# Gate and up of the second FFN: two pairs of blocks by seven part products in place of eight (Strassen's algorithm)

## The chip, the cores and the metric

The kernel runs on one core of one Trainium2 chip. Its time is the device time of one execution in microseconds; the median of the runs is quoted. Engines are named as in the profile: PE is TensorE (PEld its weight loads), DVE is VectorE, ACT is ScalarE, POOL is GpSimd, SP issues the DMAs.

## What is computed

One decoder layer on 256 tokens of width 1024, in float32: an FFN, a mixing layer (attention and a gated unit side by side), a second FFN, and a last normalization. The second FFN, cut to what matters:

```python
def swiglu(x, w_gu, w_down):
    g, u = jnp.split(x @ w_gu, 2, axis=-1)        # w_gu (1024, 2*2816)
    return (jax.nn.silu(g) * u) @ w_down          # w_down (2816, 1024)
...
y = modulate(rmsnorm(h, norm_ffn2[l]), sh3, sc3)  # y (256, 1024)
h = h + 0.5 * gt3[:, None, :] * swiglu(y, w_ffn2_gu[l], w_ffn2_down[l])
return rmsnorm(h, norm_final)
```

## The kernel before

Every large product is made of three matmuls in the fp32r format: each operand is split into a high part (rounded to fp32r, by a copy on ACT) and a low part (the rest, by a subtraction on DVE), and high x high, low x high and high x low are summed in PSUM. So each weight tile of 128 x 1024 (512 KB) is loaded by SP into one of 8 `raw` buffers (`RBUFS`), copied by ACT into one of 10 `wh` buffers, and subtracted by DVE into one of 10 `wl` buffers (`WBUFS`; `add_weight`, lines 193 to 207). A `raw` buffer comes free with the subtraction, a `wh` and `wl` pair with the last matmul that reads it.

The hidden width 2816 is worked in 11 blocks of 256. A block's gate and up weights are four such tiles (kq 0 to 3), each with two slices of the contraction by 512 columns (256 gate, 256 up); its down weights are two tiles. Blocks 0 and 1 of the second FFN are computed with tokens stationary and 512 weight columns moving (`k_part`, `step_g`). From block 2 on, `gate_up` (line 461) has the weights stationary, 128 columns at a time, and the 256 tokens moving, so that gate and up lie in PSUM with the hidden index on the partitions: 96 matmuls of 256 columns a block. `act` (line 439) applies SiLU on ACT and multiplies on DVE; `turn` (line 447), called inside the next block, splits the result into the units `ah` and `al`. Where a block's activations are kept by token tile (blocks 0 and 1; a dictionary), `turn` first transposes them on PE, four transposes of 128 x 128. `down` (line 487) then adds 24 matmuls of 512 columns into four output banks. The order is gate and up of block b, then down of block b-2, from block 2 to 9; block 10 has no down stage, and the down stages of blocks 8 to 10 come last, with the residual and the final normalization.

Small tiles are units of 128 x 512 floats from one pool (`UNITS`). PSUM has four accumulators, and two banks each in the pools `psm` and `pst`, which the blocks use in turn.

Each engine runs its own queue in order. The order in which the splits of weights, and side work (`fill`: the modulation rows), are put between the matmuls is set while the kernel is built: `tick` (line 321), called after each few matmuls, issues the next item as long as the planned time of DVE is less than `LEAD` (1 us) ahead of that of PE, fewer than 10 weight tiles are live, and, while side work is left, fewer than `AHEAD` (4) tiles are unused (`fillers`, line 327). The planned times are the columns of each instruction over a rate (`Paced`). An item not yet issued when a matmul needs it is issued there (`need`).

Of the kernel before, what the change touches and what calls it, by code (L numbers as in the profile page):

```python
# [8 lines left out]
F32 = mybir.dt.float32  # L9
F32R = mybir.dt.float32r  # L10
AF = mybir.ActivationFunctionType
ALU = mybir.AluOpType
AX = mybir.AxisListType

P = 128
D = 1024
# [4 lines left out]
NB = FF // 256  # L21
# [3 lines left out]
NEG = -1e30  # L25
NFIRST = 4
FW = NFIRST * 256
UNITS = 22
WBUFS = 10
RBUFS = 8  # L30
HOLD = 3
AHEAD = 4
LEAD = 1
GAP = 3
DOWNS = {4: (0, 1), 5: (2, 3), 6: (4,), 7: (5,), 8: (6,), 9: (7,)}
# [66 lines left out]
def tile_decoder_layer(ctx: ExitStack, tc, i, out):  # L102

    nc = tc.nc
    vec, ten = Paced(nc.vector, _vector_cost), Paced(nc.tensor, _tensor_cost)
    wp = ctx.enter_context(tc.tile_pool(name="wp", bufs=WBUFS))
    const = ctx.enter_context(tc.tile_pool(name="const", bufs=1))
    sm = ctx.enter_context(tc.tile_pool(name="sm", bufs=4))
    opening = ExitStack()
    op = opening.enter_context(tc.tile_pool(name="opening", bufs=4))  # L110
# [7 lines left out]
    def unit(name, shape, dtype=F32):  # L118

        return units[0].tile(shape, dtype, tag="u", name=name)  # L120
# [3 lines left out]
    def open_units():  # L124
        opening.close()
        units.append(ctx.enter_context(tc.tile_pool(name="u2", bufs=UNITS)))

# [6 lines left out]
    def pst(name):  # L134
        return ps_tr.tile([P, 512], F32, tag="tr", name=name)

    def tsl(t):
        return slice(t * P, (t + 1) * P)
# [2 lines left out]
        return slice(n * 512, (n + 1) * 512)  # L141


    c_one = const.tile([1, D], F32, name="c_one")
    cols = const.tile([P, 88], F32, name="cols")
    h = [const.tile([P, D], F32, name=f"h{t}") for t in range(NT)]
    nc.scalar.dma_start(cols, i["cols"])
# [17 lines left out]
    for n in range(2):  # L165
        p = pst(f"pc{n}")
# [22 lines left out]
    weights, fill = [], []  # L189
    ready, unused, live = {}, set(), set()  # L190
    keep, fill_at, auto = [0], [0.0], [False]

    def add_weight(key, srcs, shape, n=1024):
        def run():
            nm = "_".join(str(x) for x in key)
            raw = wp.tile([P, 1024], F32, tag="raw", name=f"raw_{nm}", bufs=RBUFS)
            wh = wp.tile([P, 1024], F32R, tag="wh", name=f"wh_{nm}")
            wl = wp.tile([P, 1024], F32R, tag="wl", name=f"wl_{nm}")
            for view, src in srcs(raw[:, :n]):
                nc.sync.dma_start(view, src)  # L200
            nc.scalar.activation(wh[:, :n], raw[:, :n], AF.Copy)  # L201
            vec.tensor_tensor(wl[:, :n], raw[:, :n], wh[:, :n].bitcast(F32), op=ALU.subtract)
            ready[key] = (shape(wh[:, :n]), shape(wl[:, :n]))
            unused.add(key)
            live.add(key)

        weights.append((key, run))

    def gu_item(tag, w, b, kq):
        def srcs(raw):  # L210
            yield raw, w[b, kq]
        add_weight((tag, b, kq), srcs, lambda t: t.rearrange("p (k n) -> p k n", k=2))
# [6 lines left out]
    def rows_item(tag, w, b, k):  # L219
# [2 lines left out]
            yield raw, w[r0:r0 + P, :]  # L222
        add_weight((tag, b, k), srcs, lambda t: t)

    adaacc, adahl, adarow = {}, {}, {}
    spare = [pst]

    GATES = (2, 5, 8)

# [76 lines left out]
    def upto(items, key):  # L306

        while any(k == key for k, _ in items):
            items.pop(0)[1]()

    def done(key):

        live.discard(key)

    def need(key):
        if key not in ready:
            upto(weights, key)
        unused.discard(key)
        return ready[key]

    def tick():
        vec.t = max(vec.t, ten.t)
        while auto[0] and vec.t < ten.t + LEAD:
            if not fillers(1):
                return

    def fillers(n):
        for _ in range(n):
            w = weights and len(live) < WBUFS
            f = len(fill) > keep[0] and ten.t >= fill_at[0]  # L330
            if w and (len(unused) < AHEAD or not f):
                weights.pop(0)[1]()
            elif f:
                if fill[0][0][0] == "ada":
                    fill_at[0] = max(fill_at[0], ten.t) + GAP
                fill.pop(0)[1]()
            else:
                return False
        return True
# [22 lines left out]
    yh = const.tile([P, KT, S], F32R, name="yh")  # L362
    yl = const.tile([P, KT, S], F32R, name="yl")
# [56 lines left out]
    def run(ops, n=None):  # L420
        for _ in range(len(ops) if n is None else min(n, len(ops))):
            ops.pop(0)()
            tick()


    class Ffn:
# [20 lines left out]
        def turn(self, b):  # L447

            pv = self.pa[b]
            if isinstance(pv, dict):  # L450
                pv = pst(f"pa_{self.name}{b}").rearrange("p (k n) -> p k n", k=2)
                for t in range(NT):
                    for k in range(2):
                        ten.transpose(pv[:, k, tsl(t)], self.pa[b][t][:, tsl(k)], ident)
            ah = unit(f"ah_{self.name}{b}", [P, 2, S], F32R)
            al = unit(f"al_{self.name}{b}", [P, 2, S], F32R)
            nc.scalar.activation(ah, pv, AF.Copy)
            vec.tensor_tensor(al, pv, ah.bitcast(F32), op=ALU.subtract)
            self.a[b] = (ah, al)

        def gate_up(self, b, turns=()):
            get, spare[0] = (psm, pst) if b % 2 == 0 else (pst, psm)
            banks = [get(f"p{q}{self.name}{b}").rearrange("p (c n) -> p c n", c=2) for q in "gu"]
            turns = list(turns)
            for kq in range(4):
                wh, wl = need(("gu" + self.name, b, kq))
                for k in range(2):
                    kk = kq * 2 + k
                    for q in range(2):
                        for c in range(2):  # L470
                            cs = slice(q * 256 + c * P, q * 256 + c * P + P)
                            mm3w(banks[q], c, wh[:, k, cs], wl[:, k, cs], yh[:, kk, :], yl[:, kk, :], kk == 0, kk == KT - 1)
                    if turns and kq:
                        self.turn(turns.pop(0))
                done(("gu" + self.name, b, kq))
            self.act(b, *banks)
            spare[0] = pst
            assert not turns

# [14 lines left out]
    class Chain:  # L494
# [24 lines left out]
        def turn(self, n, scol, shcol):  # L519
            p = transposed(self.z[n], f"{self.name}{self.t}{n}")  # L520
            y = unit(f"y_{self.name}{self.t}{n}", [P, 4, P])
            for k in range(4):
                kk = n * 4 + k
                sc, sh = scol[:, kk:kk + 1], shcol[:, kk:kk + 1]
                nc.scalar.activation(y[:, k, :], p[:, tsl(k)], AF.Identity, scale=sc, bias=sh)
            ks = slice(n * 4, n * 4 + 4)
            dh, dl = yh[:, ks, tsl(self.t)], yl[:, ks, tsl(self.t)]
            nc.scalar.activation(dh, y, AF.Copy)
            vec.tensor_tensor(dl, y, dh.bitcast(F32), op=ALU.subtract)
# [3 lines left out]
    gu2, d2 = i["gu2"], i["w_ffn2_down"][0]  # L533
    def gu_plan(tag, b):
        return [(tag, b, kq) for kq in range(4)]

    def row_plan(tag, bs):
        return [(tag, b, k) for b in bs for k in range(2)]

    plan = []  # L540
# [16 lines left out]
    def put(e):  # L557
        if e[0] == "gu1":
            gu_item("gu1", gu1, e[1], e[2])
        elif e[0] == "gu2":  # L560
            gu_item("gu2", gu2, e[1], e[2])
        elif e[0] == "d1":
            rows_item("d1", d1, e[1], e[2])
        elif e[0] == "d2":
            rows_item("d2", d2, e[1], e[2])
        elif e[0] == "wo":
            rows_item("wo", w_out, e[1], e[2])
        elif e[0] == "in":
            cols_item("in" + e[1], w_in, e[2], e[3])
    for name, c in (("q", 0), ("k", 1), ("v", 2), ("gv", 4), ("gu", 3)):  # L570
        plan += [("in", name, c, kq) for kq in range(4)]
    plan += row_plan("wo", range(4))
    for b in range(NB):
        plan += gu_plan("gu2", b)
        if 2 <= b <= NB - HOLD + 1:
            plan += row_plan("d2", (b - 2,))
    plan += row_plan("d2", range(NB - HOLD, NB))
    for e in plan:
        put(e)
# [159 lines left out]
    for e in OPEN.split():  # L739
        e = e.split(".")  # L740
        steps[e[0]](*[int(x) if x.isdigit() else x for x in e[1:]])
    auto[0] = True
    waiting = list(FORDER)
# [11 lines left out]
    f2 = Ffn("2")  # L755
# [140 lines left out]
    gated, p_gate, attn, attn_r, gate_r = {}, {}, {}, {}, {}  # L896
# [28 lines left out]
    probs, sums = {}, {}  # L925
# [121 lines left out]
    for e in MIX.split():  # L1047
        if e == "w":
            owed[0] += 1
        else:  # L1050
            e = e.split(".")
# [3 lines left out]
            step_w()  # L1055
    auto[0] = True
    keep[0] = 0
    waiting = [0, 1]
    for b in range(2, NB):
        f2.gate_up(b, waiting)  # L1060
        waiting = [b]
        if b <= NB - HOLD + 1:
            f2.down(b - 2)
    last = waiting.pop()
    for b in waiting:
        f2.turn(b)
# [2 lines left out]
    for t in range(NT):  # L1069
        c = Chain(t, "z")  # L1070
        z = [unit(f"zo{t}{n}", [P, 512]) for n in range(2)]
# [19 lines left out]
        if apart:  # L1091
            for q in range(2):
                o = slice(q * 256, q * 256 + 256)
                pe = psm(f"pe{q}")[:, 0:256]
                for k in range(2):
                    ah, al = f2.a[last]
                    wh, wl = need(("d2", last, k))
# [65 lines left out]
```

## Time and profile before

| | |
|---|---|
| median of 3 runs | 505.31 us (505.19 to 505.74) |
| the profiled execution, its own time | 505.38 us |
| its span, first to last instruction | 503.7 us |
| PE / DVE / ACT / POOL busy | 492.3 / 372.8 / 263.5 / 23.9 us |
| mean granted TensorE clock | 0.997 of 2.4 GHz |
| HBM traffic | 124.91 MB read, 1.05 MB written |

The span is what the trace covers; the rest of the execution's time lies around it. Busy times are sums over an engine's instructions. Matmuls overlap, so that one takes longer from start to end than the distance to the next start; it is these distances that add up to time.

### The profile page before, as it was taken

Reading aid. Unit: us, or ns where it says so; the run is one execution under the profiler, and the core shown is the slowest. Engines: PE = TensorE matmul, PEld = TensorE weight load, DVE = VectorE, ACT = ScalarE, POOL = GpSimd, SP = SyncE. Lnnn points to the kernel's source line nnn. Section 1 sums busy time; section 2 is a strip of 40 time slices with the busy share of each in tenths; the row PEclk is TensorE's granted clock in tenths of the full one; section 3 lists DMA queues with packets and bytes.
Section 4 is the critical chain, followed back from the end, with each engine's and each line's share of the span. In section 5 each row is a group of like instructions: output and inputs, shape, how many; then the busy total and the mean of one; then the engine's idle time right before and its main releaser. Section 6 shows DMA issues by size and latency. Waiting matters only on the chain.

```text
span 503.7 us, 8140 instructions
## 1 busy us (share of the span) xinstructions
PE 492.3 (98%) x3159; PEld 443.6 (88%) x3159; DVE 372.8 (74%) x491; ACT 263.5 (52%) x386; POOL 23.9 (5%) x36
## 2 busy tenths in 40 slices
PE   8999999999999999999999999999999999999993
PEld 6999999899999997878788888899899999999983
DVE  5999989888788557799888899779645454554245
ACT  5566774544444345775685457854543444435122
POOL 4000000000000200100002220000000000000000
PEclk9999999999999999999999999999999999999998
DMA  8999979999999965569696667789956555640002
GB/s 291 403 399 397 389 240 371 395 375 314 313 316 341 333 234 200 181 204 330 212 319 210 220 212 279 234 323 325 337 178 204 169 195 179 188 149 0 1 1 85
DMA packets 38025, 126.50 MB, mean 251 GB/s; under 512 B 4449, under 2 KB 4449, under 8 KB 37986
## 3 DMA queue, kind: packets, MB, share of 16 engines
q1 hardware_dynamic: 37458, 125.39, 70.4%
q8 instruction: 25, 0.41, 0.3%
q10 hardware_dynamic: 432, 0.57, 0.3%
q14 instruction: 14, 0.11, 0.1%
q0 software_dynamic: 96, 0.01, 0.0%
HBM read 124.91 MB, written 1.05 MB: 250 GB/s over the span
## 4 chain that ended last, share of the span: by engine, by line
PE 91%; DMA 3%; DVE 2%; issue 2%; ACT 1%; SPq 0%; POOL 0%; POOLq 0%; ACTq 0%
PE pg L80 23%; PE po L80 22%; PE pu L80 18%; PE f L80 6%; PE pw L80 4%; DMA raw_first<-in_gu_dram 3%; PE pp_gv L80 2%; PE pp_v L80 2%; PE pp_k L80 2%; PE pp_q L80 2%; PE pp_gu L80 2%; PE psc L80 2%; PE pv L80 1%; DVE wl_first L80 1%; PE pada L80 1%
## 5 line engine op out<-in xcount | busy, mean ns | idle before, releaser
L80 DVE TENSOR_TENSOR wl_gu<-raw_gu,wh_gu 128x1024 fp32r<-128x1024 f32 x72 | 87.1, 1223 | 41.3 <-ACT wh_gu L201 41.1
L201 ACT ACTIVATE wh_gu<-raw_gu 128x1024 fp32r<-128x1024 f32 x72 | 74.9, 1057 | 56.3 <-PE po L80 38.4
L80 DVE TENSOR_TENSOR wl_d<-raw_d,wh_d 128x1024 fp32r<-128x1024 f32 x44 | 53.7, 1223 | 30.7 <-ACT wh_d L201 28.8
L80 PE MATMUL pu<-yh,wl_gu 128*128 128x256 f32 x256 | 72.8, 284 | 0.0
L80 PE MATMUL pg<-yh,wl_gu 128*128 128x256 f32 x256 | 72.7, 284 | 0.0
L80 PE MATMUL pu<-yl,wh_gu 128*128 128x256 f32 x256 | 72.5, 283 | 0.0
L80 PE MATMUL pg<-yl,wh_gu 128*128 128x256 f32 x256 | 72.5, 283 | 0.0
L80 PE MATMUL pu<-yh,wh_gu 128*128 128x256 f32 x256 | 72.2, 282 | 0.2 <-DVE a L80 0.2
L80 PE MATMUL pg<-yh,wh_gu 128*128 128x256 f32 x256 | 72.2, 282 | 0.0
L201 ACT ACTIVATE wh_d<-raw_d 128x1024 fp32r<-128x1024 f32 x44 | 46.3, 1058 | 47.9 <-PE pu L80 22.3
L80 PE MATMUL po<-wh_d,ah 128*128 128x512 f32 x174 | 68.5, 394 | 0.0
L80 PE MATMUL po<-wl_d,ah 128*128 128x512 f32 x174 | 68.4, 393 | 0.0
L80 PE MATMUL po<-wh_d,al 128*128 128x512 f32 x174 | 67.8, 390 | 0.0
L80 PEld LDWEIGHTS pg<-yh,wh_gu 128*128 128x128 f32 x256 | 48.5, 189 | 0.6
L80 PEld LDWEIGHTS pu<-yh,wh_gu 128*128 128x128 f32 x256 | 48.5, 190 | 0.5 <-DVE a L80 0.4
L80 PEld LDWEIGHTS pg<-yl,wh_gu 128*128 128x128 f32 x256 | 48.2, 188 | 0.7
L80 PEld LDWEIGHTS pu<-yh,wl_gu 128*128 128x128 f32 x256 | 48.3, 189 | 0.0
L80 PEld LDWEIGHTS pg<-yh,wl_gu 128*128 128x128 f32 x256 | 48.3, 189 | 0.0
L80 PEld LDWEIGHTS pu<-yl,wh_gu 128*128 128x128 f32 x256 | 48.2, 188 | 0.0
L80 PEld LDWEIGHTS po<-wh_d,al 128*128 128x128 f32 x174 | 32.7, 188 | 7.4
L80 PEld LDWEIGHTS po<-wh_d,ah 128*128 128x128 f32 x174 | 32.7, 188 | 6.7
L80 DVE SCALAR_TENSOR_TENSOR ada<-ada,c_row 128x1024 f32<-128x1024 f32 x32 | 38.6, 1219 | 0.0
(226 smaller groups left out, 884.9 us busy)
## 6 DMA issues: line engine op xcount, KB each, us to landing
raw_gu<-in_gu_dram SPq DMA_DIRECT2D x72, 512.0 KB, 4.9
raw_d<-in_w_ffn_down_dram SPq DMA_DIRECT2D x44, 512.0 KB, 4.7
ada<-in_w_shsc_dram SPq DMA_DIRECT2D x32, 512.0 KB, 5.1
ada<-in_w_gate_dram SPq DMA_DIRECT2D x24, 512.0 KB, 4.9
raw_ada<-in_w_shsc_dram SPq DMA_DIRECT2D x16, 512.0 KB, 7.1
raw_first<-in_gu_dram SPq DMA_DIRECT2D x16, 512.0 KB, 7.4
raw_wo<-in_w_out_dram SPq DMA_DIRECT2D x8, 512.0 KB, 4.4
raw_inq<-in_w_in_dram SPq DMA_DIRECT2D x4, 512.0 KB, 5.6
```

The lines of the kernel that those rows point to most:

```text
L80: return getattr(self.engine, name)(out, *args, **kw)
L201: nc.scalar.activation(wh[:, :n], raw[:, :n], AF.Copy)
```

## The change

Blocks 5 and 6, and blocks 8 and 9, become two pairs. For a pair, the 256 tokens are cut into two tiles of 128, the contraction into two halves of 512, and the columns are the two blocks of 512 (gate and up of each). Of this 2 x 2 x 2 product, seven part products are computed in place of eight: each has one of the activations or of four sums of them (`sum_y`, made once, in blocks 2 to 4, from the activations before their split, which are therefore kept) against one of the weight quarters "11", "12", "21", "22" or of combinations of them. The combinations are made in the `raw` buffers by eight subtractions a pair on DVE (`minus`), and every product's weights, two tiles, are split like others. A pair so holds all eight `raw` buffers, and has 14 tiles to split in place of 8. Products are added into banks where they can be; where a bank goes on to be added to, its sum so far is copied out by ACT (`u1`, `u2`, `u3`). The gated activations of a pair lie by token tile, and so go through the transposes of `turn`. The down stages of the two blocks before come inside the pair, one after the fifth product and one at the end.

Beside it: 24 units in place of 22, `c_one` in a pool that closes early, weights of a pair issued up to 10 tiles ahead whether side work is left or not, and no gate row (`adar`) inside a pair's products. The diff, without some smaller plumbing:

```diff
@@ -25,11 +25,13 @@
-UNITS = 22
+UNITS = 24
+PAIRS = (5, 8)
+STRASSEN = ("P1", "P5", "P6", "P2", "P7", "P3", "P4")
...
-    c_one = const.tile([1, D], F32, name="c_one")
+    c_one = op.tile([1, D], F32, name="c_one", bufs=1)
...
+    def add_pair(tag, w, b, extra):
+        part = {}
+        def load(name, blk, half):
+            for q in range(2):
+                part[name, q] = wp.tile([P, 1024], F32, tag="raw", name=f"raw_{tag}_{b}{name}{q}", bufs=RBUFS)
+                nc.sync.dma_start(part[name, q], w[blk, half * 2 + q])
+        high = {}
+        def hi(name, key, q):
+            high[key, q] = wp.tile([P, 1024], F32R, tag="wh", name=f"wh_{tag}_{b}{key}{q}")
+            nc.scalar.activation(high[key, q], part[name, q], AF.Copy)
+        def lo(name, key, q):
+            raw, wh = part[name, q], high[key, q]
+            wl = wp.tile([P, 1024], F32R, tag="wl", name=f"wl_{tag}_{b}{key}{q}")
+            vec.tensor_tensor(wl, raw, wh.bitcast(F32), op=ALU.subtract)
+            k = (tag, b, key, q)
+            ready[k] = tuple(t.rearrange("p (k n) -> p k n", k=2) for t in (wh, wl))
+            unused.add(k)
+            live.add(k)
+        def minus(to, x, y, q):
+            vec.tensor_tensor(part[to, q], part[x, q], part[y, q], op=ALU.subtract)
+        def prep(key, q):
+            if q == 0 and key in ("P1", "P5", "P6", "P2"):
+                load(*{"P1": ("11", b, 0), "P5": ("12", b + 1, 0), "P6": ("22", b + 1, 1), "P2": ("21", b, 1)}[key])
+            if key == "P5":
+                minus("11", "12", "11", q)
+            elif key == "P6":
+                minus("12", "22", "12", q)
+                minus("11", "22", "11", q)
+            hi(place[key], key, q)
+        place = dict(zip(STRASSEN, ("11", "11", "11", "21", "12", "22", "21")))
+        order = [(key, q) for key in STRASSEN for q in range(2)]
+        def item(n):
+            def run():
+                if n == 0:
+                    prep(*order[0])
+                if n + 1 < len(order):
+                    prep(*order[n + 1])
+                key, q = order[n]
+                lo(place[key], key, q)
+                if key == "P2":
+                    minus("21", "21", "11", q)
+            return run
+        for n, (key, q) in enumerate(order):
+            weights.append(((tag, b, key, q), item(n)))
+            x = {9: 0, 13: 1}.get(n)
+            if x is not None and extra[x] is not None:
+                for e in row_plan("d2", (extra[x],)):
+                    put(e)
...
-            f = len(fill) > keep[0] and ten.t >= fill_at[0]
-            if w and (len(unused) < AHEAD or not f):
+            f = len(fill) > keep[0] and ten.t >= fill_at[0] and not (no_rows[0] and fill[0][0][0] == "adar")
+            ahead = WBUFS if w and weights[0][0][-2] in STRASSEN else AHEAD
+            if w and (len(unused) < ahead or not f):
...
-        def gate_up(self, b, turns=()):
+        def gate_up(self, b, turns=(), sums=()):
...
+                if sums and kq in (1, 2):
+                    sum_y(sums.pop(0))
+            for m in sums:
+                sum_y(m)
...
+        def pair(self, b, turns, downs):
+            tag, n = "gu" + self.name, f"{self.name}{b}"
+            turns = list(turns)
+            half = [slice(0, 4), slice(4, 8)]
+            def y(t, k):
+                return yh[:, half[k], tsl(t)], yl[:, half[k], tsl(t)]
+            def prod(bank, ops, key, fresh):
+                for q in range(2):
+                    wh, wl = need((tag, b, key, q))
+                    for k in range(2):
+                        st, sp, kk = fresh and q + k == 0, q + k == 2, q * 2 + k
+                        for x, (m, w) in enumerate(((0, wh), (1, wh), (0, wl))):
+                            ten.matmul(bank, ops[m][:, kk, :], w[:, k, :], start=st and x == 0, stop=sp and x == 2,
+                                       skip_group_check=not fresh)
+                        tick()
+                    done((tag, b, key, q))
+            def copy(bank, name):
+                u = unit(f"{name}_{n}", [P, 512])
+                nc.scalar.activation(u, bank, AF.Copy)
+                return u
+            def gated(blk, t, u, x):
+                nc.scalar.activation(u[:, 0:256], x[:, 0:256], AF.Silu)
+                vec.tensor_tensor(u[:, 0:256], u[:, 0:256], x[:, 256:512], op=ALU.mult)
+                self.pa.setdefault(blk, {})[t] = u[:, 0:256]
+            def summed(blk, t, u, bank):
+                vec.tensor_tensor(u, u, bank, op=ALU.add)
+                gated(blk, t, u, u)
+            no_rows[0] = True
+            get, spare[0] = (psm, pst) if b % 2 == 0 else (pst, psm)
+            pa, pc = get(f"pA{n}"), get(f"pC{n}")
+            prod(pa, y(0, 0), "P1", True)
+            u1 = copy(pa, "u1")
+            if turns:
+                self.turn(turns.pop(0))
+            prod(pc, sums_y[1], "P5", True)
+            if turns:
+                self.turn(turns.pop(0))
+            prod(pa, sums_y[2], "P6", False)
+            u2 = copy(pa, "u2")
+            pb = spare[0](f"pB{n}")
+            prod(pb, y(0, 1), "P2", True)
+            summed(b, 0, u1, pb)
+            prod(pa, sums_y[3], "P7", False)
+            u3 = copy(pa, "u3")
+            summed(b + 1, 1, u3, pc)
+            no_rows[0] = False
+            if downs[0] is not None:
+                self.down(downs[0])
+            no_rows[0] = True
+            prod(pc, sums_y[4], "P3", False)
+            summed(b + 1, 0, u2, pc)
+            prod(pa, y(1, 1), "P4", False)
+            gated(b, 1, unit(f"u4_{n}", [P, 512]), pa)
+            no_rows[0] = False
+            if downs[1] is not None:
+                self.down(downs[1])
...
+            if self.name == "f":
+                y_part[self.t, n] = y
...
+        if b in PAIRS:
+            plan.append(("pair", b))
+        elif b - 1 not in PAIRS:
+            plan += gu_plan("gu2", b)
+            if 2 <= b <= NB - HOLD + 1:
+                plan += row_plan("d2", (b - 2,))
...
+    def sum_y(m):
+        to, x, y, o = {1: ((1, 1), (1, 0), (1, 1), ALU.add), 3: ((1, 0), (0, 0), (1, 0), ALU.subtract),
+                       2: ((0, 0), (1, 1), (0, 0), ALU.subtract), 4: ((0, 1), (0, 1), (0, 0), ALU.subtract)}[m]
+        z = y_part[to]
+        vec.tensor_tensor(z, y_part[x], y_part[y], op=o)
+        zh, zl = (unit(f"s{m}{q}", [P, 4, P], F32R) for q in "hl")
+        nc.scalar.activation(zh, z, AF.Copy)
+        vec.tensor_tensor(zl, z, zh.bitcast(F32), op=ALU.subtract)
+        sums_y[m] = (zh, zl)
     waiting = [0, 1]
+    due = {2: [1], 3: [3], 4: [2, 4]} if min(PAIRS) > 4 else {2: [1, 3], 3: [2, 4]}
     for b in range(2, NB):
-        f2.gate_up(b, waiting)
-        waiting = [b]
-        if b <= NB - HOLD + 1:
-            f2.down(b - 2)
+        if b in PAIRS:
+            f2.pair(b, waiting, pair_downs(b))
+            waiting = [b, b + 1]
+        elif b - 1 not in PAIRS:
+            f2.gate_up(b, waiting, due.get(b, []))
+            waiting = [b]
+            if b <= NB - HOLD + 1:
+                f2.down(b - 2)
```

## Rows read from the trace of the kernel before

**Rows 1.** The page: span, and busy time, share and instructions of each engine.

```profile
span 503.7 us, 8140 instructions
PE 492.3 (98%) x3159; PEld 443.6 (88%) x3159; DVE 372.8 (74%) x491; ACT 263.5 (52%) x386; POOL 23.9 (5%) x36
```

**Rows 2.** Windows, blocks 3, 4, 4 to 9, 10: length; busy; clock; DMA.

```profile
347.10:365.30 18.20, 18.20 (x126) 16.69 (x125) 12.69 (x13) 9.73 (x12) 0.00 (x0) 1.00 0.94 346
365.30:382.40 17.10, 17.10 (x122) 16.10 (x121) 8.64 (x8) 7.48 (x8) 0.00 (x0) 1.00 0.59 189
...
365.30:467.60 102.30, 102.30 (x723) 96.28 (x722) 51.85 (x48) 44.89 (x48) 0.00 (x0) 1.00 0.48 155
467.60:479.10 11.50, 11.50 (x97) 11.50 (x97) 1.83 (x2) 2.18 (x3) 0.00 (x0) 1.00 0.01 1
```

**Rows 3.** Waits in blocks 4 to 9: total us, times, longest.

```profile
DVE wl_gu L80 <- ACT wh_gu L201: 27.0, 21, 1.7
ACT wh_gu L201 <- PE po L80: 19.2, 11, 1.8
DVE wl_d L80 <- ACT wh_d L201: 19.1, 15, 1.7
```

**Rows 4.** Timeline of VectorE, block 6: start, us, instruction, [idle before].

```profile
400.66 1.23 DVE L80 TENSOR_TENSOR wl_gu<-raw_gu,wh_gu 128x1024 fp32r<-128x1024 f32 x1 [1.52 <-ACT wh_gu L201]
403.41 1.23 DVE L80 TENSOR_TENSOR wl_d<-raw_d,wh_d 128x1024 fp32r<-128x1024 f32 x1 [1.53 <-ACT wh_d L201]
...
406.29 1.22 DVE L80 TENSOR_TENSOR wl_d<-raw_d,wh_d 128x1024 fp32r<-128x1024 f32 x1 [1.05 <-ACT wh_d L201]
409.17 1.23 DVE L80 TENSOR_TENSOR wl_gu<-raw_gu,wh_gu 128x1024 fp32r<-128x1024 f32 x1 [1.66 <-ACT wh_gu L201]
```

**Rows 5.** Timeline of TensorE: block 5's first matmul, and its down stage's ends.

```profile
382.29 0.28 PE L80 MATMUL pg<-yh,wh_gu 128*128 128x256 f32 x1
...
393.81 0.40 PE L80 MATMUL po<-wh_d,ah 128*128 128x512 f32 x1
...
399.32 0.28 PE L80 MATMUL pg<-yh,wh_gu 128*128 128x256 f32 x1
```

**Rows 6.** TensorE's timeline, blocks 0, 1: second of 66 matmuls; block 2's first.

```profile
313.75 0.39 PE L80 MATMUL pg<-wh_gu,yl 128*128 128x512 f32 x1
...
328.85 0.28 PE L80 MATMUL pg<-yh,wh_gu 128*128 128x256 f32 x1
```

**Rows 7.** Timeline of TensorE in block 2: an early block's turn.

```profile
333.50 0.28 PE L80 MATMUL pu<-yh,wl_gu 128*128 128x256 f32 x1
333.61 0.60 PE L80 MATMUL pa<-ident,a 128*128 128x128 f32 x4
333.97 0.36 PE L80 MATMUL pg<-yh,wh_gu 128*128 128x256 f32 x1
334.17 0.28 PE L80 MATMUL pg<-yl,wh_gu 128*128 128x256 f32 x1
```

**Rows 8.** Groups by line and form from 325 us: busy, mean ns | idle.

```profile
L80 DVE TENSOR_TENSOR wl_gu<-raw_gu,wh_gu 128x1024 fp32r<-128x1024 f32 x31 | 37.8, 1224 | 32.4 <-ACT wh_gu L201 32.4
L201 ACT ACTIVATE wh_gu<-raw_gu 128x1024 fp32r<-128x1024 f32 x31 | 32.6, 1060 | 34.2 <-PE po L80 24.6 <-PE pu L80 9.3
L80 DVE TENSOR_TENSOR h<-h,res_z 128x512 f32<-128x512 f32 x4 | 2.8, 692 | 0.1
L443 ACT ACTIVATE sg<-pg 128x512 f32<-128x512 f32 x9 | 5.4, 599 | 18.0 <-PE pg L80 18.0
L80 DVE TENSOR_TENSOR a<-sg,pg 128x256 f32<-128x256 f32 x2 | 0.8, 422 | 1.1 <-ACT sg L435 1.1
```

**Rows 9.** The page: DMA issues, KB each, median us from issue to landing.

```profile
raw_d<-in_w_ffn_down_dram SPq DMA_DIRECT2D x44, 512.0 KB, 4.7
```

**Rows 10.** Timeline of TensorE: a wait in block 2, and the last gate row.

```profile
329.95 0.39 PE L80 MATMUL pu<-yh,wh_gu 128*128 128x256 f32 x1 [0.23 <-DVE a L80]
...
356.57 0.50 PE L80 MATMUL pada<-accl,onesr 128*128 128x512 f32 x1
```

More of the change, by code (lines that the diff above doesn't have):

```diff
@@ L225, in tile_decoder_layer @@
     adaacc, adahl, adarow = {}, {}, {}
-    spare = [pst]
+    spare, no_rows, sums_y, y_part = [pst], [False], {}, {}
     GATES = (2, 5, 8)
@@ L450, in turn @@
             if isinstance(pv, dict):
-                pv = pst(f"pa_{self.name}{b}").rearrange("p (k n) -> p k n", k=2)
+                pv = spare[0](f"pa_{self.name}{b}").rearrange("p (k n) -> p k n", k=2)
                 for t in range(NT):
@@ L475, in gate_up @@
                 done(("gu" + self.name, b, kq))
+                if sums and kq in (1, 2):
+                    sum_y(sums.pop(0))
+            for m in sums:
+                sum_y(m)
             self.act(b, *banks)
+            spare[0] = pst
+            assert not turns
+        def pair(self, b, turns, downs):
[54 more added lines that the diff above has]
+                self.down(downs[1])
@@ L561, in put @@
             gu_item("gu2", gu2, e[1], e[2])
+        elif e[0] == "pair":
+            add_pair("gu2", gu2, e[1], pair_downs(e[1]))
         elif e[0] == "d1":
@@ L572, in tile_decoder_layer, with pair_downs @@
     plan += row_plan("wo", range(4))
+    def pair_downs(b):
+        return tuple(x if x < NB - HOLD else None for x in (b - 2, b - 1))
     for b in range(NB):
-        plan += gu_plan("gu2", b)
-        if 2 <= b <= NB - HOLD + 1:
-            plan += row_plan("d2", (b - 2,))
+        if b in PAIRS:
[4 more added lines that the diff above has]
+                plan += row_plan("d2", (b - 2,))
     plan += row_plan("d2", range(NB - HOLD, NB))
```

## The prediction

> **What bounds the kernel now.** I read the busy times first: TensorE is busy for 492.3 of 503.7 us, VectorE for 372.8, ScalarE for 263.5 [rows 1]. By blocks of the second FFN, blocks 4 to 9 (six blocks, 102.3 us) have TensorE busy throughout at a granted clock of 1.00, the upper level of 2.4 GHz, while VectorE works 51.85 us and ScalarE 44.89 us of it [rows 2]. So here time is TensorE's time alone, and what an edit is worth is the matmul time it takes off, unless VectorE or ScalarE come to make TensorE wait. Why VectorE idles half of that stretch shows in the waits: the low split waits for ScalarE's high split, which waits for a matmul to give its buffer back [rows 3]. Inside one block the low splits come some 2.8 us apart with 1.05 to 1.66 us of idleness before each [rows 4]. The two engines are held back by the ten weight buffers, always about ten tiles ahead of TensorE: a cushion and a reserve, both of which this change draws on.
>
> The sum is made against the profiled execution: 505.38 us (span 503.7 and 1.68 around it); the median of the runs shown is 505.31.
>
> **Matmuls of a pair, before.** Block 5's gate and up run from 382.29 to 393.81 us: 96 matmuls of 256 columns in 11.52 us, 0.1200 us each; the 24 of 512 columns of a down stage take 5.51 us, 0.2296 each [rows 5]. Two blocks: 192 x 0.1200 = 23.04 us.
>
> **After.** A product is 4 slices of the contraction (512 of 1024) by 3 matmuls, tokens stationary, 512 weight columns moving: 12 matmuls, 84 for seven products. The trace has this very form, in blocks 0 and 1: from 313.75 to 328.85 us lie 65 issues, 0.2323 us each [rows 6]. The down stage's 0.2296 is the other end, but it writes two banks in turn, three matmuls each; blocks 0 and 1 write six into one bank in a row, as a product does. I take 0.2323: 84 x 0.2323 = 19.51 us, 3.53 off per pair, 7.06 for two (with 0.2296: 19.29, 3.75, 7.51). Of this, an eighth of the old time, 2.88 us per pair, is the eighth product; the other 0.65 is that 512 columns in one matmul cost less than twice 256.
>
> The Trainium skill would make this less: its page "TensorE: Matmul & The Clock Gate" (section Back-to-back issue gap) gives 262 cycles for 256 columns and 518 for 512, which at 2.4 GHz I estimate as 109.2 and 215.8 ns. By that the pair saves 20.96 - 18.13 = 2.84 us, and the kernel would end near 501.5, an estimate too. The rows above disagree with both figures (120.0 and 232.3 ns).
>
> **Transposes.** A pair leaves its gated activations with tokens on the partitions, so each of its blocks needs four transposes in `turn`, which the blocks before did without. The turns of blocks 0 and 1, whose activations lie so too, show the price: 0.36 us from its first transpose to the next matmul, and that matmul's successor comes 0.20 instead of 0.12 us later: 0.44 [rows 7]. Four turns: 1.75 us, all on TensorE, inside blocks 7 and 10. They wait for nothing: the last of a pair's activations has the next down stage (5.51 us) and a quarter of a block to be finished.
>
> **Sum on TensorE:** -7.06 + 1.75 = -5.31 us, so 505.38 - 5.31 = 500.07. With the other rate 499.62.
>
> **VectorE.** A weight split costs 1.225 us, an operation of 512 columns 0.69, of 256 columns 0.42 [rows 8]. Per pair there are 14 low splits for 8 and 8 subtractions of the same shape (the nearest row is the split itself): 14 x 1.225 = 17.15 us more. Three sums with a bank and four products of 256 columns replace two of 512: 2.07 + 1.69 - 1.38 = 2.38 more. The four sums of activations (blocks 2 to 4) are 8 x 0.69 = 5.5 us, half of it in block 4. The stretch of blocks 4 to 9 would hold 51.85 + 2 x 19.53 + 2.8 = 93.7 us of VectorE work in 102.3 - 7.06 + 0.88 = 96.1 us. That is 97%, and so the whole question. Two things relieve it. The last six splits of the down weights (7.35 us) need not be done in that stretch: in block 10 VectorE works 1.83 of 11.5 us [rows 2]. And a pair's 10 tiles for P1 to P7 (as the code orders them) are split ahead, while the down stages inside a pair use two tiles each in 5.51 us.
>
> By due times, from the start of block 4 (time 0): P1 is due at 17.0, P5 19.8, P6 22.6, P2 25.4, P7 28.2, down 31.0, P3 36.5, P4 39.3, the next down 42.0, block 7 at 47.6. At time 0 P1 and P5 are split, if VectorE used the idle 5.5 us of block 3 (18.20 - 12.69, [rows 2]) for one activation sum and two subtractions (3.8). Then up to P7 stand 12 operations of 1.225 (14.7), two activation sums (2.8) and the gating of blocks 3 and 4 (1.4): 18.9, two of lateness make 20.9, against 28.2. After it each tile costs 1.225 with 1.1 for a sum and a gating: 25 against 31.0, 29 against 36.5, 31 against 39.3, 35 against 42.0. The cushion never falls below 6 us; the second pair, with block 7 ahead of it and no activation sums there, is alike or better. I price VectorE's added work at nothing; without that cushion it would be up to 2 x 19.5 us.
>
> **ScalarE** gets 6 more high splits (6.4 us), three copies of a bank (1.8) and 0.4 of shorter gatings per pair; it works 7.48 of 17.1 us per block [rows 2]. Nothing, on load. Its order counts more: the copy of the bank after P1 must be read before P6 adds to that bank, 2.79 us (P5) later, and so again after P6, before P7. The copy takes 0.60 us, like the gating's row [rows 8]. It stands in ScalarE's queue behind whatever split was issued ahead of it.
>
> **Weights' DMA.** The same 16 tiles per pair of blocks come in, so traffic is equal. But a pair holds all eight raw buffers; the next down stage's first tile loads only when "11" is free, after P2's split and the last subtraction, by the ledger about 15.2 us after block 4's start. Landing takes 4.7 us [rows 9]: 19.9, or 2.9 after P1 began. Its split on ScalarE (1.06) may stand just ahead of the copy after P1 (ready at 19.8): the copy would end at 21.6, and P6 is due at 22.6. This is the thinnest margin in the change, 1.0 us; every us more of lateness there is a us of TensorE, once per pair. I take 0; the upper bound is a whole landing per pair, 2 x 4.7.
>
> **Other edits.** Two more units, the activations kept for the sums (4 units) and the eight units of sums reach no row; a shorter reuse distance costs between 0 and one wait like the one TensorE has at block 2 for an activation, 0.23 us [rows 10]. `c_one` in another pool, the changed filler test and the ban on the gate rows during a pair touch work that ends near 357 us [rows 10], ahead of the first pair: nothing, at most one such wait.
>
> **Rivals.**
> - *Fed with small stalls.* The copies after P1 and P6 come late, because a split waiting for its DMA or a subtraction is ahead in the queue. For it: the 1.0 us of margin, and that each idle of VectorE in [rows 4] ends on ScalarE. Against it: the ledger. One half to a third of a landing per pair, 1 to 3.3 us in all: 501.1 to 503.4.
> - *VectorE sets the pace (slower).* Blocks 4 to 9 show 46.1 us of VectorE waiting for ScalarE before 36 splits, 1.28 each [rows 3, 4]. If the chain of subtraction, high split, low split keeps such a wait before 24 of the pairs' 44 low splits and subtractions, that is 30.7 us on top of 86.4 (93.7 less the 7.35 that may slip): 117.1 against 96.1. The cushion and block 10's idleness, about 13 us by estimate, pay for part, 8.0 stay: 500.1 + 8.0 = 508.1. It decides where those waits exceed some 28 us (the 5.3 gained beyond 96.1 + 13 - 86.4 = 22.7), 22 of them. Against it: the waits of now are for buffers, and there is slack in them, not a latency. The Trainium skill's same page (section Architectural detail: the array is 16× 32×32) says that ScalarE and VectorE queues are strict first-in first-out, which this rival needs; the trace agrees in that a low split waits while nothing overtakes it [rows 4].
> - *No gain from longer matmuls.* A product's matmul costs twice one of 256 columns, 0.2400 us [rows 5], and only the eighth product is saved: 2 x 2.88 - 1.75 = 4.01, 501.4. Against it: [rows 6]. The gaps of the Trainium skill, above, come to nearly this.
> - *It does not do what it says*: a product's matmuls take as long as an eighth of before (3.29 us), for instance waiting on weight loads; then only the transposes are left: 507.1. [Rows 6] speak against it.
>
> **From this the numbers.** Chances: fed as computed 0.60 (own range 499.4 to 501.0), small stalls 0.24, no gain from longer matmuls 0.03, VectorE's pace 0.07, not as said 0.02, and 0.04 for stalls that just eat the gain. A run of this kernel tells about 0.2% (1.0 us) from no change: faster means below 504.3 (0.60 + 0.24 + 0.03 = 0.87), slower above 506.3 (0.09), same 0.04. Forecast 500.1; the range 499.2 to 503.4 holds the first three cases but for their tails, and leaves under 2 in 10 out.
>
> **What would show it.** Right: seven runs of 12 matmuls of 512 columns in 2.79 us each with no TensorE idleness between them; four transposes twice in blocks 7 and 10; blocks 5 to 10 shorter by about 5.3 us and all ahead of block 2 unchanged; VectorE over 90% busy in blocks 5 to 9. Wrong: TensorE waiting for a low split (VectorE's pace), or for the copy of a bank ahead of P6 or P7 (queue order), or a product well off 2.79 us.

## The result, and the profile after

The changed kernel takes 500.92 us (median of four runs, 500.41 to 501.33) against 505.25 before; the ratio is 0.9911, interval 0.9900 to 0.9923. That is 4.3 us faster, where the forecast (505.38 to 500.1) was 5.3; the time lies inside the range and at the upper edge of what was given for the case without waits.

The page after, busy times, against [rows 1]:

```profile
span 499.2 us, 7816 instructions
PE 487.7 (98%) x2959; PEld 431.6 (86%) x2959; DVE 411.6 (82%) x537; ACT 277.9 (56%) x412; POOL 23.6 (5%) x36
```

TensorE has 200 matmuls fewer, VectorE 38.8 us more work. By stages after (block 3 with its down stage, block 4, first pair, block 7, second pair, block 10; length, then busy time of PE, PEld, DVE, ACT, POOL, granted clock, DMA):

```profile
346.90:364.10 17.20, 17.20 (x122) 16.16 (x121) 15.04 (x17) 8.38 (x11) 0.00 (x0) 1.00 0.79 303
364.10:381.10 17.00, 17.00 (x121) 16.02 (x120) 14.98 (x17) 8.26 (x11) 0.00 (x0) 1.00 0.00 1
381.10:412.90 31.80, 31.73 (x138) 25.52 (x137) 27.09 (x28) 21.16 (x28) 0.00 (x0) 1.00 0.83 289
412.90:431.70 18.80, 18.48 (x129) 16.76 (x128) 18.17 (x19) 9.00 (x12) 0.00 (x0) 1.00 0.13 44
431.70:462.20 30.50, 30.50 (x133) 24.83 (x133) 26.90 (x29) 21.13 (x26) 0.00 (x0) 1.00 0.68 241
462.20:474.50 12.30, 12.30 (x106) 12.29 (x105) 3.57 (x4) 2.79 (x4) 0.00 (x0) 1.00 0.00 0
```

Where [rows 2] had VectorE busy for 8.64 of 17.1 us a block, it now works 15.0 of 17.0 in block 4 and 18.2 of 18.8 in block 7. In the rows of the first pair and of block 7 TensorE's busy time is below the length: there it waits. From the starts of the stages in the two traces, in us (the last stage is followed by the same tail, 24.7 us):

| | before | after | difference | forecast |
|---|---|---|---|---|
| start of block 5 | 382.29 | 381.14 | -1.15 | 0 |
| blocks 5 and 6 | 34.05 | 31.74 | -2.31 | -3.53 |
| block 7 | 17.03 | 18.87 | +1.84 | +0.88 |
| blocks 8 and 9 | 34.05 | 30.46 | -3.59 | -3.53 |
| block 10, gate and up | 11.52 | 12.27 | +0.75 | +0.88 |
| sum | | | -4.46 | -5.30 |

The first two rows belong together: the last gate row (`pada`, four matmuls) left block 3 (1.17 us there) for the first pair's down stage (0.92 us). Without it, and without a wait of 0.34 us, the first pair is 30.48 us: as good as the second.

TensorE's timeline after, at the two joints where it waited longest: from P2 to P7 in the first pair, and the down stage in block 7. Columns: start, us, instruction, [idle before].

```profile
392.09 0.40 PE L82 MATMUL pB<-wl_gu_5P,yh 128*128 128x512 f32 x1
392.56 0.50 PE L82 MATMUL pA<-wh_gu_5P,s3h 128*128 128x512 f32 x1
392.89 0.39 PE L82 MATMUL pA<-wh_gu_5P,s3l 128*128 128x512 f32 x1
393.12 0.39 PE L82 MATMUL pA<-wl_gu_5P,s3h 128*128 128x512 f32 x1
...
425.39 0.28 PE L82 MATMUL pu<-yh,wl_gu 128*128 128x256 f32 x1
425.87 0.50 PE L82 MATMUL po<-wh_d,ah 128*128 128x512 f32 x1 [0.20 <-ACT ah L522]
426.21 0.39 PE L82 MATMUL po<-wl_d,ah 128*128 128x512 f32 x1
426.59 0.50 PE L82 MATMUL po<-wh_d,al 128*128 128x512 f32 x1
426.93 0.39 PE L82 MATMUL po<-wh_d,ah 128*128 128x512 f32 x1
```

A wait need not stand in the brackets: the sign is the distance of starts. P7's first starts 0.47 us after its neighbour, the next 0.33, where 0.2323 is usual: 0.34 lost. At the down stage the four distances are 0.48, 0.34, 0.38 and 0.34; at the same joint of block 4 the first is 0.12, since the matmul ahead of it has 256 columns, and the others are 0.23: 0.72 lost. A third wait lies at 413.86, where block 7's second bank waits for the last gating of the pair (VectorE ends it at 413.81): 0.28, and 0.10 more at the next start, 0.38. Together the three are 1.44 us.

What made P7 late is in ScalarE's timeline after; `u<-pA` is the copy of the bank after P6:

```profile
386.54 1.06 ACT L203 ACTIVATE wh_d<-raw_d 128x1024 fp32r<-128x1024 f32 x1 [1.29 <-DMA raw_d<-in_w_ffn_down_dram]
389.06 1.06 ACT L203 ACTIVATE wh_d<-raw_d 128x1024 fp32r<-128x1024 f32 x1 [1.46 <-DMA raw_d<-in_w_ffn_down_dram]
390.03 1.99 ACT L242 ACTIVATE wh_gu_5P<-raw_gu 128x1024 fp32r<-128x1024 f32 x2
391.92 0.58 ACT L571 ACTIVATE u<-pA 128x512 f32<-128x512 f32 x1
```

P6 was done at about 389.7, the copy could have run then; it stood behind a split that waited for its tile to land, and two more. And the down stage in block 7, the same engine later:

```profile
417.45 1.06 ACT L242 ACTIVATE wh_gu_8P<-raw_gu 128x1024 fp32r<-128x1024 f32 x1 [1.33 <-DVE raw_gu L82]
420.86 1.06 ACT L242 ACTIVATE wh_gu_8P<-raw_gu 128x1024 fp32r<-128x1024 f32 x1 [2.35 <-DVE raw_gu L82]
424.27 1.06 ACT L242 ACTIVATE wh_gu_8P<-raw_gu 128x1024 fp32r<-128x1024 f32 x1 [2.35 <-DVE raw_gu L82]
425.23 1.07 ACT L522 ACTIVATE ah<-pa 128x512 fp32r<-128x512 f32 x2
```

The transposed activations of blocks 5 and 6 had been ready from 418 and 420 us on. Their splits (`ah`) stand behind high splits of the next pair, each of which waits 1.3 to 2.4 us for a subtraction on VectorE, with ScalarE idle.

### The profile page after: what moved, and what is told of

Its sections match the earlier page's. It is cut to its first block, busy times and chain, and to the rows that moved or that the text cites. A ratio compares the mean times of both kernels' runs of the same rounds, so it can differ in the third digit from the quotient of the medians.

```text
span 499.2 us, 7816 instructions
## 1 busy us (share of the span) xinstructions
PE 487.7 (98%) x2959; PEld 431.6 (86%) x2959; DVE 411.6 (82%) x537; ACT 277.9 (56%) x412; POOL 23.6 (5%) x36
## 4 chain that ended last, share of the span: by engine, by line
PE 83%; DVE 7%; issue 4%; ACT 3%; DMA 3%; POOL 0%; POOLq 0%; ACTq 0%; DVEq 0%; SPq 0%
PE po L82 19%; PE pg L82 17%; PE pu L82 13%; PE f L82 6%; PE pw L82 4%; PE pA L82 3%; PE pp_gv L82 2%; PE pp_v L82 2%; PE pp_q L82 2%; PE pp_k L82 2%; PE pp_gu L82 2%; PE psc L82 2%; DMA raw_first<-in_gu_dram 2%; DVE raw_gu L82 1%; DVE wl_gu_5P L82 1%
## 5 line engine op out<-in xcount | busy, mean ns | idle before, releaser
L82 DVE TENSOR_TENSOR wl_gu<-raw_gu,wh_gu 128x1024 fp32r<-128x1024 f32 x56 | 66.9, 1221 | 11.5 <-ACT wh_gu L203 11.3
L203 ACT ACTIVATE wh_gu<-raw_gu 128x1024 fp32r<-128x1024 f32 x56 | 57.3, 1054 | 25.0 <-PE po L82 15.3
L82 PE MATMUL pu<-yh,wh_gu 128*128 128x256 f32 x192 | 54.3, 283 | 0.3 <-DVE a L82 0.2
L82 PE MATMUL pg<-yh,wh_gu 128*128 128x256 f32 x192 | 54.5, 284 | 0.0
L82 PE MATMUL pu<-yh,wl_gu 128*128 128x256 f32 x192 | 54.4, 283 | 0.0
L82 PE MATMUL pg<-yh,wl_gu 128*128 128x256 f32 x192 | 54.4, 283 | 0.0
L82 PE MATMUL pu<-yl,wh_gu 128*128 128x256 f32 x192 | 54.2, 283 | 0.0
L82 PE MATMUL pg<-yl,wh_gu 128*128 128x256 f32 x192 | 54.2, 282 | 0.0
L82 PEld LDWEIGHTS po<-wl_d,ah 128*128 128x128 f32 x174 | 32.7, 188 | 6.6
L82 PEld LDWEIGHTS pu<-yh,wh_gu 128*128 128x128 f32 x192 | 36.3, 189 | 0.8 <-DVE a L82 0.4
```

Source lines behind the costliest of these rows:

```text
L82: return getattr(self.engine, name)(out, *args, **kw)
```

## The experiments

Medians are given beside 505.3 to 505.4 us of the kernel before on the same chip; where an edit is short it stands as a diff against the changed kernel.

**Eight products in the pair's form** (against the kernel before; `gate_up_tok` calls `k_part` for both token tiles, then `act_t`):

```diff
-        f2.gate_up(b, waiting)
+        (f2.gate_up_tok if b in (5, 6, 8, 9) else f2.gate_up)(b, waiting)
```

> Blocks 5, 6, 8 and 9 in the form of the pair's matmuls (tokens stationary, 512 columns moving, gating by token tile, transposes in the next block), but with all eight products: no sums, no subtractions, eight weight tiles. Theory (the form alone is worth 96 x 0.2323 = 22.30 against 23.04 us per two blocks, and costs 0.88 of transposes): 0.28 us over the kernel before, 505.5, that is no measurable change, and the eighth product is all that pays. Rival (the longer matmuls are the larger part of the gain, or the transposes cost less than 0.44 each): under 504.5.

Measured 505.41 us, ratio 1.0001 (0.9992 to 1.0010): the theory's 505.5. The longer matmuls pay just for the transposes; what the change gains is the eighth product.

**One pair:**

```diff
-PAIRS = (5, 8)
+PAIRS = (8,)
```

> Only blocks 8 and 9 are a pair; 5 and 6 stay as in the kernel before. Theory (the gain is a sum of terms per pair, 3.53 us of matmul less 0.88 of transposes, and what is lost to waits is lost in the first pair and in block 7, which lies between two pairs): 2.65 us off the kernel before, 502.6, and no wait of TensorE in blocks 7 to 9, since block 7 then has neither late splits nor transposes ahead of its down stage. Rival (each pair brings its own waits, about half of the 1.2 us that the two lose): 503.2.

Measured 503.07 us, ratio 0.9956 (0.9942 to 0.9969), nearer to the rival's number, but not by its reason. Blocks 8 and 9 take 30.46 us, as in the changed kernel, and nothing waits in blocks 7 to 9. The excess is in block 3, where the gate row stayed:

```profile
358.70 0.51 PE L82 MATMUL pada<-accl,onesr 128*128 128x512 f32 x1 [0.39 <-DVE accl L82]
```

The row's split comes later on VectorE than before (its activation sum of block 3 lies ahead), and block 5 starts at 382.88 in place of 382.29 us: 0.59. -3.59 + 0.75 + 0.59 = -2.25, that is 503.1. Neither theory had this wait in it.

**No subtractions:**

```diff
-            vec.tensor_tensor(part[to, q], part[x, q], part[y, q], op=ALU.subtract)
+            vec.t += _vector_cost("tensor_tensor", part[to, q], ())
```

> Both pairs, without the 16 subtractions that form the weight combinations (the products are taken with the plain quarters); the order of everything else is kept. It takes 19.6 us of work from VectorE. Theory (TensorE's three waits all come from VectorE being behind: ScalarE's high splits wait for a subtraction, and a copy or a split of activations stands behind them): the waits go, 1.2 us less than the changed kernel, 499.7. Rival (the waits are those of weights' landing and of ScalarE's own order): 500.9 as it is.

Measured 499.75 us, ratio 0.9890 (0.9876 to 0.9903): the theory's 499.7. Nowhere from block 3 to 10 does TensorE wait any more. The run does not tell VectorE's load from the landing of weights, since it changes both: with buffer "11" free earlier, SP issues the load of the first down tile inside the pair at 369.50 in place of 383.17 us. *Nine raw buffers* and *Transposes earlier* tell them apart.

**Splits doubled:**

```diff
             vec.tensor_tensor(wl, raw, wh.bitcast(F32), op=ALU.subtract)
+            if key in ("P1", "P5", "P6"):
+                nc.vector.tensor_tensor(wl, raw, wh.bitcast(F32), op=ALU.subtract)
```

> Both pairs, with the low split of the products P1, P5 and P6 done twice: 12 more operations of 1.22 us on VectorE, 14.7 us, nothing else changed. It looks for the point from which VectorE sets the pace. Theory (VectorE has 11 us of idle time left in the 95 us from block 4 to the second pair's end, and is already late in parts of it, so that about half of the added work turns into waits): 5 to 9 us over the changed kernel, 506 to 510. Rival 1 (the ten tiles of cushion swallow it): within 1.5 us of the changed kernel. Rival 2 (VectorE already sets the pace): all of it, 515.6.

Measured 514.17 us, ratio 1.0176 (1.0157 to 1.0195). 13.25 of the 14.7 us added come through: in number close to rival 2, but not by its reason. TensorE's waits in this kernel (total us, times, longest), and two windows of it:

```profile
PE pA L82 <- ACT u L573: 5.3, 2, 3.8
PE po L82 <- ACT ah L524: 3.9, 1, 3.9
PE po L82 <- DVE al L82: 0.3, 1, 0.3
```

```profile
394.50:403.00 8.50, 4.68 (x14) 3.61 (x14) 7.53 (x8) 4.94 (x7) 0.00 (x0) 0.80 0.88 312
...
432.00:441.00 9.00, 4.81 (x18) 3.31 (x17) 8.93 (x10) 4.41 (x6) 0.00 (x0) 0.81 0.01 2
```

P7 and the down stage in block 7 wait as in the changed kernel, P6 (1.47 us, for the copy after P1) is new; 9.5 us in all. The clock adds some 3 us: after the waits of 3.8 and 3.9 us matmuls start 0.43 us apart for a while, at 1.2 GHz, and the granted clock of the two windows is 0.80 and 0.81. By stages the first pair grows by 7.2 us and block 7 by 5.0, the second pair and block 10 not at all. Without the clock that is about 5.5 and 3.7 us of waits for 7.35 us of splits added to each pair: 9 of 14.7, the upper end of the theory's 5 to 9, and the clock, which the theory left out, carries it to rival 2's number. All of these waits are for copies and splits of activations and none for a product's low split, whose smallest lead over its matmul falls from 6.5 us in the changed kernel to 3.2.

**Three pairs:**

```diff
-PAIRS = (5, 8)
+PAIRS = (5, 7, 9)
```

> Blocks 5 and 6, 7 and 8, 9 and 10 as three pairs in a row, so that no plain block stands between them. On TensorE alone a third pair is worth 3.53 less 0.88 us: 498.3. Theory (VectorE is at its limit: a pair asks 36 us of it in 30.5 us of matmuls, and block 7, where it caught up, is gone): about 5.5 us of waits in each of the second and third pair, 508 to 510, and the clock of TensorE falls behind the longest of them. Rival (the ten tiles of cushion carry it): under 500.

Measured 511.17 us, ratio 1.0116 (1.0102 to 1.0130), a little worse than the theory, and not where it had the waits. VectorE is busy for 31.2 of 34.0 us (412 to 446) and 31.95 of 38.0, and in the third pair single products wait for their low splits. A window that holds the third pair, and two of TensorE's waits:

```profile
446.00:484.00 38.00, 31.33 (x128) 23.08 (x126) 31.95 (x35) 21.13 (x29) 0.00 (x0) 0.96 0.35 111
```

```profile
PE pA L82 <- ACT u L571: 2.5, 2, 2.3
...
PE pA L82 <- DVE wl_gu_9P L82: 1.7, 2, 1.0
```

From the starts of the stages, the second pair loses 0.8 us, the third 8.7 (34.45 us for work of 25.7) and the down stages behind it 4.3. The low splits' smallest lead over their matmuls shrinks from 6.3 us in the first pair to 0.2 in the second and 0.05 in the third: the second pair lives on the cushion that the blocks before the pairs had built. After the wait of 2.3 us the clock falls, as expected: it is 0.50 from 454.7 to 458.0. A pair costs VectorE more time than it leaves TensorE; a plain block between two pairs is what pays for it.

**Transposes earlier:**

```diff
-                    if turns and kq:
+                    if turns and (kq or (k and len(turns) > 1)):
```

> Both pairs; in blocks 7 and 10 the transposes of the pair's two blocks stand a slice of the contraction earlier, so that ScalarE's split of the first block's activations stands ahead of one more high split that waits for a subtraction. Theory (the wait ahead of the down stage in block 7, 0.6 us, is this split standing behind four high splits, each held by VectorE): that wait goes, 500.3, and the other two waits stay. Rival (VectorE's low split of the activations is as late by itself): 500.9.

Measured 500.52 us (ratio 0.9901, 0.9887 to 0.9914), 0.4 below the changed kernel. The first split of the activations now runs at 421.55, 3.7 us earlier, and the down stage in block 7 no longer waits; the waits at P7 and at block 7's second bank stay, and in the second pair starts 0.33 to 0.34 us apart show three small ones, 0.1 us each: 0.72 less 0.3 is the 0.4. (The edit also moves block 2's two turns, which changes no wait there.)

```profile
420.59 1.06 ACT L242 ACTIVATE wh_gu_8P<-raw_gu 128x1024 fp32r<-128x1024 f32 x1 [2.34 <-DVE raw_gu L82]
421.55 0.58 ACT L522 ACTIVATE ah<-pa 128x512 fp32r<-128x512 f32 x1
```

**Nine raw buffers:**

```diff
-UNITS = 24
+UNITS = 23
-RBUFS = 8
+RBUFS = 9
```

> Both pairs with nine raw buffers in place of eight (23 units in place of 24 make the room). A pair then no longer holds all of them, and the first down tile inside the pair can be loaded before the last subtraction. Theory (the wait of 0.34 us ahead of P7 is the copy of the bank standing behind a split that waits for that tile's landing): this wait goes, 500.6. Rival (the copy stands behind splits that VectorE delays): 500.9.

Measured 500.2 us (ratio 0.9899, 0.9883 to 0.9914), 0.7 below. The first down tile inside the pair is there when its turn comes, and the copy after P6 waits for P6 alone:

```profile
384.88 1.05 ACT L203 ACTIVATE wh_d<-raw_d 128x1024 fp32r<-128x1024 f32 x1
386.31 1.06 ACT L203 ACTIVATE wh_d<-raw_d 128x1024 fp32r<-128x1024 f32 x1 [0.37 <-DMA raw_d<-in_w_ffn_down_dram]
387.27 1.99 ACT L242 ACTIVATE wh_gu_5P<-raw_gu 128x1024 fp32r<-128x1024 f32 x2
389.52 0.60 ACT L571 ACTIVATE u<-pA 128x512 f32<-128x512 f32 x1 [0.26 <-PE pA L82]
```

P7 starts without a wait; more than that was not expected, but the wait at block 7's second bank is gone too, and 0.34 and 0.38 make the 0.7. In the changed kernel VectorE idles for 0.65 us at 390.16, until the second down tile is split high; here it does not, and the last gating of the pair runs at 412.44 in place of 413.39, ahead of the second bank's first matmul. The wait of the down stage in block 7 stays. VectorE has the same work as before, so the landing behind the pair's buffers is what half of the 1.44 us hang on.

**A subtraction on GpSimd:**

```diff
-                minus("12", "22", "12", q)
+                nc.gpsimd.tensor_tensor(part["12", q], part["22", q], part["12", q], op=ALU.subtract)
```

> Both pairs; the subtraction that makes 12 into 22 - 12 (two per pair, needed only for P7) runs on GpSimd, which does nothing in this stretch. It takes 4 x 1.22 us from VectorE. Theory (the waits come from VectorE being behind by a few us): the waits in block 7 go, 500.1 or a little less. Rival 1 (GpSimd is so much slower, or slows VectorE beside it so much, that the product P7 or the splits come later than before): 501.5 and more. Rival 2 (the waits have nothing to do with VectorE's load): 500.9.

Measured 504.7 us (ratio 0.9985, 0.9976 to 0.9993): rival 1. One of the four, with the split of VectorE ahead of it, from the timelines of GpSimd and VectorE:

```profile
363.41 3.26 POOL L263 TENSOR_TENSOR raw_gu<-raw_gu,raw_gu 128x1024 f32<-128x1024 f32 x1 [52.62 <-DVE raw_gu L82]
```

```profile
363.19 1.22 DVE L82 TENSOR_TENSOR wl_gu_5P<-raw_gu,wh_gu_5P 128x1024 fp32r<-128x1024 f32 x1
364.44 3.31 DVE L82 TENSOR_TENSOR raw_gu<-raw_gu,raw_gu 128x1024 f32<-128x1024 f32 x1
```

VectorE's subtraction, 1.22 us elsewhere, takes 3.31: it ends at 367.75, 1.1 us after GpSimd's. VectorE loses 2.1 us each time to save 1.22. In the first pair a landing then stands ahead of the copy after P1, and P6 waits: the margin named in the prediction, at its place. ScalarE's timeline, and TensorE's, where matmuls 0.43 us apart follow:

```profile
388.05 1.06 ACT L203 ACTIVATE wh_d<-raw_d 128x1024 fp32r<-128x1024 f32 x1 [2.27 <-DMA raw_d<-in_w_ffn_down_dram]
389.01 0.58 ACT L571 ACTIVATE u<-pA 128x512 f32<-128x512 f32 x1
```

```profile
387.17 0.40 PE L82 MATMUL pC<-wl_gu_5P,s1h 128*128 128x512 f32 x1
389.64 0.50 PE L82 MATMUL pA<-wh_gu_5P,s2h 128*128 128x512 f32 x1 [2.07 <-ACT u L571]
389.98 0.41 PE L82 MATMUL pA<-wh_gu_5P,s2l 128*128 128x512 f32 x1
390.21 0.61 PE L82 MATMUL pA<-wl_gu_5P,s2h 128*128 128x512 f32 x1
390.62 0.63 PE L82 MATMUL pA<-wh_gu_5P,s2h 128*128 128x512 f32 x1
```

**Both mended** (earlier transposes and nine raw buffers):

> Both pairs, with the earlier transposes and nine raw buffers (23 units) together. If the waits that each took away are independent, as the theory has them (a copy behind a late landing; a split behind subtractions): 0.4 and 0.7 us less than the changed kernel, 499.8, which is the sum of the TensorE terms with no waits (499.6 to 500.1). Rival (a wait taken away in the first pair comes back in block 7, since VectorE's queue is the cause of both): 500.2, as with nine buffers alone.

Measured 499.76 us, ratio 0.9891 (0.9876 to 0.9905): the theory's 499.8, and the best version here, 1.2 us below the changed kernel. From the first pair to block 10 no distance of starts shows a wait of more than 0.06 us, and block 10 ends 1.47 us earlier (473.01 in place of 474.48); what follows it took 0.28 us more in this execution. Nothing was taken from VectorE: in the window 412 to 430, which holds block 7, it is busy for 16.8 of 18.0 us, and it is enough.

**Ten raw buffers:**

```diff
-UNITS = 23
-RBUFS = 9
+UNITS = 21
+RBUFS = 10
```

> The same with ten raw buffers and 21 units. Theory (with nine, no tile's landing holds up a split any more, and what is left is VectorE's own work): as with nine, 499.8. Rival (more of VectorE's lateness is the wait for tiles behind a pair's buffers): 499.4. Rival 2 (three units fewer make an activation wait for its buffer): 500.5 and more.

Measured 499.76 us, ratio 0.9886 (0.9870 to 0.9903): as with nine. There was nothing left to take away.

## Why the prediction was nearly right

- *Bound.* Right: up to block 10 the time follows TensorE, and all that TensorE waited for came from ScalarE and VectorE.
- *Products.* Right: the second pair's seven take 13.93 and 5.55 us, 19.48 against 19.51.
- *Transposes.* 0.75 us in block 10 for two turns, 0.375 each against 0.44. The part "they wait for nothing" was wrong. The transposes are done in time, but the split behind them is not, because ScalarE's queue holds high splits that wait for VectorE: 0.72 us, gone with earlier transposes. Nor is the last gating done in time for block 7's second bank: 0.38.
- *VectorE*, the step that failed: its added work was priced at nothing because the splits have a cushion. The cushion itself held. The ledger said that it "never falls below 6 us"; the smallest lead of a low split over the first matmul that reads it is 6.5 us, at P7 (split by 386.64, read at 393.12), and no product waits for a split. But VectorE ran later than the ledger. At block 4's start (364.1) only one low split of this pair was done, and the first subtraction; P5's second tile was split at 369.1. The idle time of block 3 in [rows 2] was not all to be had: with gate work and a sum of activations VectorE was busy for 15.0 of 17.2 us there, and the rest are three waits for ScalarE, 0.26 to 1.20 us. The subtraction that frees "11" ended at 383.10, 19.0 us after block 4's start, where 15.2 was the forecast:

```profile
365.68 1.22 DVE L82 TENSOR_TENSOR wl_gu_5P<-raw_gu,wh_gu_5P 128x1024 fp32r<-128x1024 f32 x1
...
381.88 1.22 DVE L82 TENSOR_TENSOR raw_gu<-raw_gu,raw_gu 128x1024 f32<-128x1024 f32 x1
...
385.42 2.35 DVE L82 TENSOR_TENSOR wl_gu_5P<-raw_gu,wh_gu_5P 128x1024 fp32r<-128x1024 f32 x2
```

  The amount of work was right: the durations of VectorE's operations sum to 44.3 us more, where 2 x 19.53 + 5.5 = 44.6 was forecast (its busy time grew by only 38.8, because back to back such operations start 1.14 us apart and take 1.22). It was busy for 72.2 of 81.1 us from block 5 to 9, 89% where over 90% was to be the sign. What the ledger lacks is the instructions that have no cushion: a copy of a bank, a split of activations, the last gating. They stand in a queue behind work that waits for VectorE, or for a buffer that VectorE frees, and TensorE needs them next. They cost 1.44 us, and the two edits of *Both mended* take that away with VectorE's work as it was.
- *Weights' DMA and ScalarE's order.* The mechanism was right and is what cost the first pair 0.34 us: a landing ahead of a copy, which was also one of the prediction's own signs of being wrong. Only the copy was another one, after P6, since the one after P1 had been issued ahead of the late split. With GpSimd the predicted one waited.
- *Gate rows.* Priced at nothing, as work ahead of the first pair; the last row moved into the pair's down stage and saved 0.25 us.
- *Sum:* -5.31, +1.44 of waits (0.34 in the first pair, 0.72 and 0.38 in block 7), -0.25 for the row, -0.26 for cheaper transposes: -4.4 against -4.46. The last two, 0.5 us together, were not counted on. Without them the time would have been about 501.4, outside the 499.4 to 501.0 of the case without waits; that it lies inside is luck.
- *Rivals.* In mechanism "small stalls" came true, in part: 1.44 us of waits, inside its 1 to 3.3 us, though two of the three stand at places that it did not name; and its 501.1 to 503.4 was missed by the 0.5 us above. "VectorE sets the pace" had its threshold too high, at 28 us of waits: 14.7 us of work added (doubled splits), or a third pair with no plain block between, made the kernel 9 and 6 us slower than before. In the last rival 3.29 us is a seventh, not an eighth, of the 23.04 us before; the argument stays.

## What to carry to other kernels

Work saved on the bounding engine and paid for on one that is half idle is not free when the second feeds the first through short queues and few buffers: look at the stages where the feeding work must be done, at what stands in each queue ahead of the instruction that the bounding engine needs next, and put such an instruction (a copy of a bank, a split of activations) ahead of prefetches that may wait. After such a change look for the distances of starts on the bounding engine that have grown by tenths of a us; here three such places, mended by one more buffer and by moving two calls, gave 1.2 us. A ledger of due times tells whether the products are fed; it has to list these single instructions too. And a change that wins twice need not win three times: the third pair, with no plain block left between, lost 10 us.

## What was not expected of the hardware

- A subtraction of 128 x 1024 floats takes GpSimd 3.26 us from start to end, and one of VectorE that runs beside it takes 3.31 in place of 1.22, ending 1.1 us after GpSimd's. The Trainium skill's page "SBUF — State Buffer" (section SBUF: two separate sides) says that the two share a pair of ports by an exclusive lock, which an instruction holds from start to end; the trace agrees, as VectorE's runs nearly its whole length after GpSimd's end. GpSimd's own 3.26 begin beside VectorE's split, which ends at 364.41; 2.26 us lie after that, in all four cases. How long GpSimd takes undisturbed no run shows.
- After the waits of 2.07 us (subtraction on GpSimd) and 3.81 us (doubled splits) TensorE's matmuls of 512 columns started 0.43 us apart for eight starts, at 1.2 GHz, beginning two and four matmuls after the wait was over: 8 x 0.2 = 1.6 us beyond the wait itself. After the waits of 2.27 us (three pairs) and 3.86 us (doubled splits) the granted clock was 0.50 from the first or second matmul on. After the 1.47 us in the doubled splits, and the 0.34 and 0.72 us in the changed kernel, matmuls started 0.23 us apart again after at most four starts.
